# Channel vectors and x in one array: a changed order and size of the first transfers of an encoder trunk, and 25 warming products instead of 21

## The chip, the cores and the metric

The kernel runs on one core of a Trainium2 chip. The metric is the device time of one execution in microseconds (us); of several executions the median is given. A core has engines that run side by side, each with its own queue of instructions: TensorE (matrix products; PE in the profile, and PEld for the loading of its weights), VectorE (DVE), ScalarE (ACT), GpSimd (POOL) and SyncE (SP), which here issues nearly all transfers from device memory into on-chip memory (SBUF). The engines wait for each other and for transfers by semaphores.

## The reference, cut to what matters

Two layers of an encoder on x of 256 rows (T) by 1024 channels (D), all in float32. Each layer is

```
h = RMSNorm(x) * g_mix
[B_a | C_a | X_a | U_p | Q | K | V | Ga | Gp | Gt] = h @ W_in
y_a = W_a_out( B_a * conv3( C_a * X_a ) )
y_p = pool_scale * blockdiag( centred means of U_p  -  U_p )
y_t = W_attn_out( windowed attention of Q, K, V )
x   = x + W_o( sig(Ga)*y_a + sig(Gp)*y_p + sig(Gt)*y_t )
x   = x + W_down( silu(h2 W_gate) * (h2 W_up) ),  h2 = RMSNorm(x) * g_ffn
```

and a last RMSNorm follows. Six vectors of 1024 channels belong to a layer: g_mix, g_ffn, the three taps of the convolution, and pool_scale. They are the "channel vectors" of this document.

## The kernel before

The activations lie transposed: x is an array of 128 partitions by 8 blocks (k = 0 to 7) of 256 rows. The weights are cut into blocks of 128 by 128, put on the host into one long list `wst` in the order in which they are used, and stream in as chunks of 16 blocks (1 MB), with three buffers `raw`. Half a chunk (8 blocks) is converted at a time: ScalarE rounds it to the type fp32r (`hi`, L136), VectorE takes the rest (`lo`, L137). An activation is split in the same way. A block then costs three products on TensorE: hi by hi (L163), hi by the activation's rest (L164), the weight's rest by hi (L165). Each is 128x128 by 128x256.

The first products of the kernel are those for K and V of layer 0 (`quad_outer`, called first in `mixer`). Its loop runs over the eight k on the outside and four column blocks inside, so one k takes 4 blocks and 12 products, and all eight take 32 blocks (chunks 0 and 1) and 96 products. Q follows with chunk 2; the first of its eight column blocks is 24 products, and behind it stand the small products of the norm (L283). The activation that enters here is x times the channel vector g_mix (`xg_tiles`): `xg` is first rounded (on VectorE at L248 for k = 0 and 1, on ScalarE at L250 for the others) and then its rest is taken on VectorE (L251). The factor of the norm is multiplied in later. Beside that, the squares of x are taken on ScalarE (L257) and added on VectorE.

Before all this TensorE multiplies a tile of zeros WARM times (`wps`, L181), with no reader.

What sets the order: on SyncE the order of the code (`dma_chunk`); on the other engines a scheduler, from the code's order and its own costs. Chunk 0 and chunk 1 come in pieces with blocks of x between them (`dma_chunk`, `c < 2`); the channel vectors `ch` come first, in a transfer of their own. SyncE's transfers use eight semaphores in turn, so the ninth transfer waits, at its issue, until the first has landed, the tenth for the second, and so on.

## Time and profile before

| | |
|---|---|
| three executions | 980.19, 980.25 and 980.49 us; median 980.25 |
| the profiled execution | 981.37 us |
| its span, first to last instruction | 979.6 us, so 1.77 us lie around it |
| TensorE busy | 969.8 us, 99% of the span, 7877 products |
| VectorE, ScalarE, GpSimd busy | 711.9, 553.4, 41.4 us |
| granted clock of TensorE | 0.998 over the span |
| moved by transfers | 178.11 MB, mean 182 GB/s |
| last of the 21 warming products starts | at 5.6 us |
| first product that counts | starts at 7.21 us |

Times in the profile count from the first instruction. The rows of the timeline give the start, the duration, the engine, the line of the kernel, and what is written from what; a number behind x counts like rows merged into one, and what stands in brackets is how long the engine was idle before, and what it waited for. "SPq" is SyncE's queue of transfers: such a row is the issue alone, the transfer lands later.

### The profile page before, as it was taken

What the parts mean: (1) busy time and instruction counts of PE and PEld (TensorE: products, weight loads), DVE (VectorE), ACT (ScalarE), POOL (GpSimd) and SP (SyncE); (2) the same over time, 40 slices, a digit from 0 to 9 for tenths busy, and PEclk for the clock granted to TensorE, in tenths of its full rate; (3) what the DMA queues carried; (4) which work ended last, traced back from release to release, by engine and by line L of the source; (5) the groups of instructions that cost most, each with busy time, mean ns of one, the idle gap of its engine ahead of it and who ended that gap; (6) DMA issues with size and microseconds to landing.
All of it is one profiled execution on the core that took longest, in us unless ns stands there. A gap on an engine that the chain in (4) does not pass through costs nothing.

```text
span 979.6 us, 19115 instructions
## 1 busy us (share of the span) xinstructions
PE 969.8 (99%) x7877; PEld 956.7 (98%) x7877; DVE 711.9 (73%) x1277; ACT 553.4 (56%) x916; POOL 41.4 (4%) x60
## 2 busy tenths in 40 slices
PE   8999999999999999999999999999999999999997
PEld 8999999999999999999999999999999999999996
DVE  7899888667668955546589888975777697555555
ACT  5866676654456544444577566765554574444443
POOL 6000000000002000000020000000000020000000
PEclk9999999999999999999999999999999999999999
DMA  8656544555554555455543745444554455545531
GB/s 299 230 192 207 184 162 160 194 177 193 183 201 171 179 181 200 179 178 195 188 173 130 248 160 181 143 170 173 185 203 173 172 194 178 209 173 188 197 132 43
DMA packets 27399, 178.11 MB, mean 182 GB/s; under 512 B 3312, under 2 KB 4096, under 8 KB 7088
## 3 DMA queue, kind: packets, MB, share of 16 engines
q1 hardware_dynamic: 25200, 169.93, 48.7%
q0 software_dynamic: 2112, 6.97, 2.5%
q8 instruction: 61, 1.00, 0.4%
q14 instruction: 26, 0.21, 0.1%
HBM read 175.80 MB, written 1.08 MB: 181 GB/s over the span
## 4 chain that ended last, share of the span: by engine, by line
PE 98%; DMA 1%; DVE 0%; ACT 0%; SPq 0%; issue 0%; DVEq 0%
PE b L164 25%; PE b L163 25%; PE b L165 25%; PE dn L165 2%; PE dn L163 2%; PE dn L164 2%; PE dn L623 2%; PE dn L622 2%; PE dn L621 2%; PE wo L163 2%; PE wo L164 2%; PE o L395 2%; PE wo L165 2%; PE pt L380 1%; PE sc L351 1%; PE sc L352 1%
## 5 line engine op out<-in xcount | busy, mean ns | idle before, releaser
L137 DVE TENSOR_TENSOR lo<-raw,hi 128x1024 fp32r<-128x1024 f32 (+1 forms) x322 | 390.0, 1219 | 208.8 <-ACT hi L136 208.3
L136 ACT ACTIVATE hi<-raw 128x1024 fp32r<-128x1024 f32 (+1 forms) x322 | 337.2, 1052 | 331.0 <-PE b L164 212.5
L163 PE MATMUL b<-h,hi 128*128 128x256 f32 x1344 | 379.8, 283 | 0.0
L165 PE MATMUL b<-h,lo 128*128 128x256 f32 x1344 | 378.4, 282 | 0.0
L164 PE MATMUL b<-h,hi 128*128 128x256 f32 x1344 | 378.3, 281 | 0.0
L164 PEld LDWEIGHTS b<-h,hi 128*128 128x128 f32 x1344 | 253.2, 188 | 0.2
L163 PEld LDWEIGHTS b<-h,hi 128*128 128x128 f32 x1344 | 253.2, 188 | 0.2
L165 PEld LDWEIGHTS b<-h,lo 128*128 128x128 f32 x1344 | 253.1, 188 | 0.0
L163 PE MATMUL b<-xg,hi 128*128 128x256 f32 x448 | 127.7, 286 | 1.2 <-DVE xg L248 1.2
L164 PE MATMUL b<-xg,hi 128*128 128x256 f32 x448 | 127.5, 285 | 0.2 <-DVE xg L251 0.2
L165 PE MATMUL b<-xg,lo 128*128 128x256 f32 x448 | 127.3, 284 | 0.0
L163 PEld LDWEIGHTS b<-xg,hi 128*128 128x128 f32 x448 | 85.6, 191 | 1.4 <-issue 1.4
L164 PEld LDWEIGHTS b<-xg,hi 128*128 128x128 f32 x448 | 85.7, 191 | 0.5 <-DVE xg L251 0.5
L165 PEld LDWEIGHTS b<-xg,lo 128*128 128x128 f32 x448 | 85.6, 191 | 0.0
L165 PE MATMUL dn<-fa,lo 128*128 128x256 f32 x176 | 49.5, 281 | 0.0
L164 PE MATMUL dn<-fa,hi 128*128 128x256 f32 x176 | 49.5, 281 | 0.0
L163 PE MATMUL dn<-fa,hi 128*128 128x256 f32 x176 | 49.5, 281 | 0.0
L364 ACT ACTIVATE s<-s,sm 128x256 f32<-128x256 f32 x64 | 31.8, 498 | 12.7 <-DVE sm L359 12.7
L163 PE MATMUL b<-z,hi 128*128 128x256 f32 x128 | 36.4, 284 | 0.0
L165 PE MATMUL b<-z,lo 128*128 128x256 f32 x128 | 36.1, 282 | 0.0
L165 PE MATMUL b<-ao,lo 128*128 128x256 f32 x128 | 36.0, 282 | 0.0
L163 PE MATMUL b<-ao,hi 128*128 128x256 f32 x128 | 36.0, 281 | 0.0
(176 smaller groups left out, 1496.6 us busy)
## 6 DMA issues: line engine op xcount, KB each, us to landing
raw<-wst SPq DMA_DIRECT2D x158, 1024.0 KB, 4.9
bias<-stab POOLq DMA_DIRECT2D x16, 384.0 KB, 4.2
raw<-wst SPq DMA_DIRECT2D x4, 256.0 KB, 5.5
raw<-wst SPq DMA_DIRECT2D x2, 512.0 KB, 6.2
out<-yg SPq DMA_DIRECT2D x4, 256.0 KB, 2.2
x<-xT SPq DMA_DIRECT2D x4, 128.0 KB, 5.4
x<-xT SPq DMA_DIRECT2D x2, 256.0 KB, 6.3
gf<-gfin POOLq DMA_DIRECT2D x2, 256.0 KB, 3.5
```

Source lines behind the costliest of these rows:

```text
L136: S.activation(hi[:, s], raw[:, s], AF.Copy)
L137: V.tensor_tensor(lo[:, s], raw[:, s], hi[:, s].bitcast(F32), op=ALU.subtract)
L163: PE.matmul(dst, wh, xh, start=start, stop=False, skip_group_check=skip)
L164: PE.matmul(dst, wh, xl, start=False, stop=False, skip_group_check=skip)
L165: last_mm[0] = PE.matmul(dst, wl, xh, start=False, stop=stop, skip_group_check=skip)
L351: PE.matmul(ps[:, half(j)], qs[t][j][:, cs], kh, start=True, stop=False)
L352: PE.matmul(ps[:, half(j)], qs[t][j][:, cs], kl, start=False, stop=True)
L364: S.activation(ss[i // 2][:, i % 2], ss[i // 2][:, i % 2], AF.Exp, bias=sm[:, 4 + i:5 + i], accum_out=sm[:, 12 + i:13 + i])
L395: PE.matmul(ps[:, half(j)], vv, pts[kt][i][:, half(j)], start=(kt == i == 0), stop=(kt == i == 1))
L621: PE.matmul(d, ah[:, cs], wh, start=(k == 0), stop=False)
L622: PE.matmul(d, ah[:, cs], wl, start=False, stop=False)
L623: PE.matmul(d, al[:, cs], wh, start=False, stop=(k == FT - 1))
```

## The change

The six channel vectors of both layers (96 numbers to a partition) are laid in front of x in one array on the host, and in one tile `xc` on the chip; `ch` and `x` become views of it. The transfer of `ch` falls away: the first transfer now brings the channel vectors and x for k = 0 together (352 numbers to a partition, 176 KB), and it is issued ahead of the first weights. The first half of chunk 0 still comes in two transfers of 4 blocks. Its second half comes in one transfer of 8 blocks instead of two of 4, and x for k = 2 and 3 in one transfer instead of two. WARM goes from 21 to 25.

```diff
+NG = L * 6 * KT
...
     def dma_chunk(c):
         raw = wp.tile([P, CT * P], F32, name=f"raw{c}", tag="raw", bufs=3)
         if c < 2:
-            if c == 0:
-                nc.sync.dma_start(ch, chp)
-            for a, b, xa, xb in (((0, 4, 0, 1), (4, 8, 1, 2), (8, 12, 2, 3), (12, 16, 3, 4)),
-                                 ((0, 8, 4, 6), (8, 16, 6, 8)))[c]:
+            for a, b, xa, xb in (((0, 4, 0, 1), (4, 8, 1, 2), (8, 16, 2, 4)), ((0, 8, 4, 6), (8, 16, 6, 8)))[c]:
+                s = slice(0 if xa == 0 else NG + xa * T, NG + xb * T)
+                if xa == 0:
+                    nc.sync.dma_start(xc[:, s], xT[:, s])
                 nc.sync.dma_start(raw[:, a * P:b * P], wst[c, :, a * P:b * P])
-                nc.sync.dma_start(x[:, xa:xb], xT[:, xa:xb])
+                if xa > 0:
+                    nc.sync.dma_start(xc[:, s], xT[:, s])
...
-    x = act.tile([P, KT, T], F32, name="x")
-    ch = const.tile([P, L, 6, KT], F32, name="ch")
+    xc = act.tile([P, NG + KT * T], F32, name="x")
+    ch = xc[:, :NG].rearrange("p (l g k) -> p l g k", l=L, g=6)
+    x = xc[:, NG:].rearrange("p (k t) -> p k t", k=KT)
...
-WARM = 21
+WARM = 25
...
+    xT = np.ascontiguousarray(np.concatenate([chp.reshape(P, NG), xT.reshape(P, KT * T)], axis=1))
```

SyncE's queue from the start of the program, before. `raw0` and `raw1` are the buffers of chunks 0 and 1; in "128x512" the second number is elements to a partition, so 128x512 is 256 KB and 128x256 is 128 KB.

```order
L120 DMA ch_104<-chp 128x96
L123 DMA raw0_105<-wst 128x512
L124 DMA x_103<-xT 128x256
L123 DMA raw0_105<-wst 128x512
L124 DMA x_103<-xT 128x256
L123 DMA raw0_105<-wst 128x512
L124 DMA x_103<-xT 128x256
L123 DMA raw0_105<-wst 128x512
L124 DMA x_103<-xT 128x256
L123 DMA raw1_115<-wst 128x1024
L124 DMA x_103<-xT 128x512
```

The same queue now:

```order
L123 DMA x_107<-xT 128x352
L124 DMA raw0_108<-wst 128x512 x2
L126 DMA x_107<-xT 128x256
L124 DMA raw0_108<-wst 128x1024
L126 DMA x_107<-xT 128x512
L124 DMA raw1_115<-wst 128x1024
L126 DMA x_107<-xT 128x512
L124 DMA raw1_115<-wst 128x1024
L126 DMA x_107<-xT 128x512
```

x for k = 0 has moved ahead of the first weights, and two transfers of 4 blocks with x between them have become one of 8 blocks; up to the first chunk of full size there are 9 transfers of x and weights in place of 13 with `ch`.

ScalarE at the same place, before. `hi0` is the first half of chunk 0, `hi1` its second half, `hi2` the first half of chunk 1; `xg3` and `xg4` belong to k = 2 and 3, `xg5` to k = 4.

```order
L136 ACTIVATE hi0_154<-raw0_105 128x512 x2
L257 ACTIVATE sq9_198<-x_103 128x512
L136 ACTIVATE hi1_166<-raw0_105 128x512
L250 ACTIVATE xg3_172<-x_103,ch_104 128x256
L136 ACTIVATE hi1_166<-raw0_105 128x512
L250 ACTIVATE xg4_175<-x_103,ch_104 128x256
L257 ACTIVATE sq10_200<-x_103 128x512
L136 ACTIVATE hi2_178<-raw1_115 128x1024
L250 ACTIVATE xg5_182<-x_103,ch_104 128x256
```

ScalarE now:

```order
L138 ACTIVATE hi0_154<-raw0_108 128x512 x2
L261 ACTIVATE sq9_198<-x_107 128x512
L138 ACTIVATE hi1_166<-raw0_108 128x512 x2
L254 ACTIVATE xg3_172<-x_107 128x256
L254 ACTIVATE xg4_175<-x_107 128x256
L261 ACTIVATE sq10_200<-x_107 128x512
L138 ACTIVATE hi2_178<-raw1_115 128x1024
L254 ACTIVATE xg5_182<-x_107 128x256
```

Both pieces of `hi1` now stand ahead of `xg3`, since both come with the one transfer. On VectorE the same pairs have changed places, and the rest of `xg1` (k = 0) now stands ahead of the first `lo0`.

TensorE, the first products, before (`b14` and `b15` are banks of sums, `xg1` is k = 0):

```order
L181 MATMUL wps_81<-warm_75 128x256 x21
L163 MATMUL b14_232<-xg1_160,hi0_154 128x256
L163 MATMUL b15_233<-xg1_160,hi0_154 128x256
L164 MATMUL b14_232<-xg1_160,hi0_154 128x256
L165 MATMUL b14_232<-xg1_160,lo0_155 128x256
```

TensorE now:

```order
L183 MATMUL wps_81<-warm_75 128x256 x25
L165 MATMUL b14_232<-xg1_160,hi0_154 128x256
L166 MATMUL b14_232<-xg1_160,hi0_154 128x256
L167 MATMUL b14_232<-xg1_160,lo0_155 128x256
L165 MATMUL b14_232<-xg1_160,hi0_154 128x256
```

The second product of k = 0 is now the one with the activation's rest, and the third the one with the weights' rest `lo0`. Further down the engines' orders are as before, product for product.

## The prediction

> **What bounds the kernel now.** I read the page first (busy times and the chain that ended last), then the chain of waits in the first 20 us, then the timeline there engine by engine.

> ```profile
> span 979.6 us, 19115 instructions
> PE 969.8 (99%) x7877; PEld 956.7 (98%) x7877; DVE 711.9 (73%) x1277; ACT 553.4 (56%) x916; POOL 41.4 (4%) x60
> PE 98%; DMA 1%; DVE 0%; ACT 0%; SPq 0%; issue 0%; DVEq 0%
> ```

> TensorE is the bound from end to end; 98% of the chain is its products. The edits touch nothing behind the first two chunks, and no product that counts is added or removed. So the change is worth what it moves the moment at which TensorE is through with K and V of layer 0; whatever is gained there is carried to the end, since the products behind it stand in the same order and follow each other without a wait. That moment is found so:

> ```profile
> 1.19 4.85 PE L181 MATMUL wps<-warm 128*128 128x256 f32 x21 [1.19 <-DVE epst L176]
> 7.21 0.76 PE L163 MATMUL b<-xg,hi 128*128 128x256 f32 x2 [1.17 <-DVE xg L248]
> 24.71 0.50 PE L283 MATMUL ps<-ones,s 128*128 128x1 f32 x4
> ```

> ```profile
> 1.66 4.95 DMA x<-xT
> 6.71 0.06 DVE xg L248
> 6.98 0.68 DVE lo L137
> 7.66 0.44 DVE xg L251
> 8.14 0.58 PE b L164
> 8.73 0.21 PE b L165
> ...
> 13.63 0.21 PE b L165
> 13.84 0.12 PE b L163
> 13.96 0.12 PE b L164
> ```

> ```profile
> 8.14:13.80 5.66, 5.66 (x27) 5.66 (x27) 5.24 (x10) 5.46 (x11) 5.60 (x14) 1.00 1.04 394
> 13.80:24.70 10.90, 10.90 (x94) 10.90 (x93) 9.06 (x12) 6.43 (x9) 5.58 (x11) 1.00 0.89 334
> ```

> The second fence is the chain of waits (start, duration, what), the third the busy times in two stretches (the first number in brackets counts products; the last three columns are granted clock, share of the transfer engines, GB/s). Two products stand at 7.21; from 8.14 on products follow without a gap: 27 at 0.21 us up to 13.8, then at 0.119 (10.9 us for the remaining 91 of the 118 that stand ahead of L283). The column of granted clock shows 1.00 in both; the spacing is the better witness: TensorE is slow until 13.8 and runs at nearly twice the pace after it. The 96 products of K and V end 24 products ahead of the 24.71, at 24.71 - 24 x 0.119 = 21.86. At full pace from 7.7 (8.14 less the two early products at 0.21) they would have ended at 19.1. So the slow start costs 2.7 us here, the late start some more.

> **What the engines ahead of TensorE do.** SyncE, then ScalarE, then VectorE:

> ```profile
> 0.74 0.39 SPq L120 DMA_DIRECT2D ch<-chp  x1
> 1.19 0.42 SPq L123 DMA_DIRECT2D raw<-wst  x1
> 1.66 0.42 SPq L124 DMA_DIRECT2D x<-xT  x1
> ...
> 5.01 0.70 SPq L123 DMA_DIRECT2D raw<-wst  x1
> 6.62 0.33 SPq L124 DMA_DIRECT2D x<-xT  x1
> 7.50 0.33 SPq L123 DMA_DIRECT2D raw<-wst  x1
> 7.87 0.43 SPq L124 DMA_DIRECT2D x<-xT  x1
> 8.68 0.33 SPq L126 DMA_DIRECT2D raw<-wst  x1
> ```

> ```profile
> 5.02 0.63 ACT L136 ACTIVATE hi<-raw 128x512 fp32r<-128x512 f32 x1 [2.77 <-DMA raw<-wst]
> 7.50 0.63 ACT L136 ACTIVATE hi<-raw 128x512 fp32r<-128x512 f32 x1 [1.85 <-DMA raw<-wst]
> ...
> 8.68 0.63 ACT L136 ACTIVATE hi<-raw 128x512 fp32r<-128x512 f32 x1
> 9.22 0.51 ACT L250 ACTIVATE xg<-x,ch 128x256 fp32r<-128x256 f32 x1
> 9.84 0.63 ACT L136 ACTIVATE hi<-raw 128x512 fp32r<-128x512 f32 x1
> 10.38 0.49 ACT L250 ACTIVATE xg<-x,ch 128x256 fp32r<-128x256 f32 x1
> 10.78 0.61 ACT L257 ACTIVATE sq<-x 128x512 f32<-128x512 f32 x1
> 11.46 1.06 ACT L136 ACTIVATE hi<-raw 128x1024 fp32r<-128x1024 f32 x1
> ```

> ```profile
> 12.55 1.23 DVE L137 TENSOR_TENSOR lo<-raw,hi 128x1024 fp32r<-128x1024 f32 x1 [0.35 <-ACT hi L136]
> 13.69 0.88 DVE L251 SCALAR_TENSOR_TENSOR xg<-x,ch,xg 128x256 fp32r<-128x256 f32 x2
> ```

> SyncE's later issues wait for landings (the issue at 5.01 for the first weights, 6.62 for the first x, 7.50 the second weights, 7.87 the second x, 8.68 the third weights), so its rows are a list of landings. In bytes ahead and included: 304 KB landed at 5.01, 432 at 6.62, 688 at 7.50, 816 at 7.87, 1072 at 8.68; the fourth weights (1456) by 9.84, when ScalarE takes them.

> **The change, part by part.**

> *x ahead of the first weights, ch with it.* Before, TensorE's start hung on x (the chain's 4.95 us), since the weights had landed 1.6 us earlier. Now x leads and the weights R end the wait. R lies between 5.0 (they are issued at the same second place, near 1.2 us) and 6.6 (the same 432 KB had landed then). From R: hi 0.63, first product at R + 0.75; the first `lo` ends 0.68 later, so the third product starts near R + 1.4 and the stream runs as if begun at R + 1.0: 6.0 to 7.6. One issue of 0.39 us falls away, hidden in R.

> *Four more warming products.* The view of the tile `wps` gives the shortest, median and longest time of one in ns, and when the first and the last start:

> ```profile
> L181 PE MATMUL wps<-warm x21: 415/415/582, 1.2 to 5.6; 128*128 128x256 f32 x21
> ```

> They follow each other at the slow pace, 4 x 0.21 = 0.85 us: the last started at 5.6, so TensorE is free at 5.8 + 0.85 = 6.7. If R is 5.0 they hold the first product back by up to 0.9 us; if R is over 5.9 they cost nothing. Together: the stream begins as if at 6.7 to 7.6, 0.1 to 1.0 us before the old 7.7. I take the middle, 7.15.

> *The clock.* This is the unknown. Before, 4.85 us of warming products did not raise the pace, then TensorE was idle for 1.17 us, and 5.7 us after 8.14 the pace rose. Now it is busy from 1.19 to 6.7 and the gap behind is at most 0.65 us plus 0.3 at the third product. Bounds: the pace rises as early as 6.9 (1.19 + 5.7), if that gap counts for nothing, and as late as the old 13.8, if products of zeros count for nothing and the phase is that of before. I take early, since the stretch of 5.5 us is nearest to the 5.7 that sufficed.

> *The second half of chunk 0 in one transfer.* By itself this is a loss: ScalarE can begin only when all 8 blocks are there. Its landing L in bytes is 176 + 256 + 256 + 128 + 512 = 1328 KB, between 1072 at 8.68 and 1456 at 9.84: 8.68 + 1.16 x 256/384 = 9.45; I take 9.4, as there are fewer and larger transfers. Bounds are 8.7 (as early as the old third) and 10.4 (where ScalarE's old `xg4` shows the last x of this chunk landed). [...]

> From L the chain is ScalarE's and VectorE's. ScalarE has the same five instructions ahead of `hi2` as before (two hi, two xg, one squares); those took from 8.68 to 11.46 = 2.78, with short waits between them that one landing removes: 2.5. From `hi2` to the rest of `xg5` (k = 4) took 11.46 to 13.69 + 0.44 = 14.13: 2.67. So k = 4 can run from L + 5.2 on. Two hi-by-hi products go ahead, 48 products belong to k = 0 to 3, so 46 of the 96 remain: 46 x 0.119 = 5.5. End of K and V = L + 5.2 + 5.5 = L + 10.65. For k = 2 the same reckoning (one hi 0.63, two `lo` of 0.65 to 0.68, the rest of `xg3` 0.44, so L + 2.4, then 70 x 0.119 = 8.3) gives L + 10.7, the same: ScalarE and VectorE make work about as fast as TensorE takes it, so this chain sets the end once the pace is high. With L = 9.4 the end is 20.05.

> Against it TensorE alone: from 7.15 at high pace at once, 96 x 0.119 = 11.4, end 18.6; with the pace rising as late as 10.3, 15 slow products, then 81 x 0.119 = 9.6, end 19.95. Both are under 20.05, so the chain through L decides for any rise up to about 10.4, and neither R nor the exact moment of the rise matters then.

> *The third chunk*, next in line:

> ```profile
> 17.52 2.01 ACT L136 ACTIVATE hi<-raw 128x1024 fp32r<-128x1024 f32 x2 [1.09 <-DMA raw<-wst]
> 18.61 2.36 DVE L137 TENSOR_TENSOR lo<-raw,hi 128x1024 fp32r<-128x1024 f32 x2 [0.43 <-ACT hi L136]
> ```

> It landed at 17.5, and its first `lo` is there at 18.61 + 1.2 = 19.8. That was 2 us ahead of its use at 21.86; now it is 0.25 us ahead of 20.05. It is late next: unless it lands earlier too, the gain stops near 2.2. The bytes ahead of it are the same, so I leave it where it was.

> *Everything else* costs nothing: the views `ch` and `x` of one tile add no wait further down, and SyncE has four issues less, which its idle time hides.

> Sum: 21.86 - 20.05 = 1.8 us. Own time of the profiled execution 981.37 - 1.8 = 979.6; the median of the runs lies 1.1 us under that execution, so 980.25 - 1.8 = 978.45.

> **The rivals.** About 0.2%, or 1.96 us, is what a measurement of this kernel can tell from no change.

> 1. *The pace rises late all the same* (12.9 to 13.8: a gap at 6.7 to 7.3 starts the count anew, or zeros don't count). From 7.15, (13.8 - 7.15)/0.213 = 31 slow products, 65 x 0.119 = 7.7, end 21.5: gain 0.4 (0.75 with 12.9), time 979.5 to 980.1. For it: 4.85 us of zeros failed before. Against it: the gap has shrunk from 1.17 us, and the stretch has grown.
> A form of it is phase: were the moment of the rise drawn anew in each execution, the new times would spread from 978.45 to 980.0, and the three before would have spread by 1 us or more; they lie within 0.30 us, so this gets 0.05 of the chance below. [...]
> 2. *The 8 blocks land early*, near 8.7, and the third chunk 0.5 us early with them, because the queues fill sooner: end 19.35, gain 2.5, time 977.7; TensorE alone would allow 18.6, a gain of 3.2. For it: the five issues up to them, 0.47 us apart, are done by 3 us, where the eight for 1456 KB took until 4.4. Against it: the stretch up to 6.6 was slow with transfers queued (432 KB landed by then).
> 3. *Slower*: the one transfer of 8 blocks starves TensorE at k = 2. The place is ScalarE's `hi1`; the price is what L exceeds 11.2 (L + 10.65 against 21.86), and for 0.2% it must exceed 13.2, though 512 KB more than L's bytes and x had been taken at 11.46 before. Even a pace that falls back in the idle time ahead of k = 2 (about 1 us, 10.5 to 11.7) and rises again at 17 gives 26 slow products, end 22.4: 0.5 us more, within 0.2%.

> **Chances.** Early pace with L between 8.9 and 10.4 (gain 0.8 to 2.3): 0.65, and within it over 1.96 us at L under 9.25, which I put at somewhat under a half: 0.28. Late pace: 0.18, phase included. Early landing: 0.12. Slower by over 0.2%: 0.03; about even or slower by less: 0.02. Faster 0.28 + 0.12 = 0.40, slower 0.03, same 0.57. The range takes in most of the late pace and most of the early landing: 977.4 to 979.95.

> **What would show it.** Right: first product at 6.7 to 7.4, spacing 0.12 from there or soon after; a gap on TensorE ahead of k = 2 (row L166 waiting for VectorE's `xg`), ScalarE's two `hi` of 128x512 back to back near 9.4; the L283 row near 22.9. Wrong: spacing 0.21 beyond 12 us (the clock step fails), `hi1` far from 9.4 (the bytes), or the L283 row moved and the end not.

## The result, and the profile after

| | before | after |
|---|---|---|
| median of four executions each | 980.22 us (980.01 to 980.49) | 987.18 us (986.86 to 988.04) |
| profiled execution, its span | 981.37, 979.6 us | 987.34, 985.2 us |
| row of the norm's products (L283, now L287) | 24.71 us | 22.96 us |
| from that row to the end of the profiled time | 956.66 us | 964.38 us |

The ratio is 1.0072, 95% interval 1.0055 to 1.009: the change made the kernel slower by 7 us, where 1.8 us of gain were forecast.

The head of the page of after: TensorE is busy for 5.6 us more than before (969.8), with only four products more.

```profile
span 985.2 us, 19117 instructions
PE 975.4 (99%) x7881; PEld 963.1 (98%) x7881; DVE 712.6 (72%) x1277; ACT 553.5 (56%) x916; POOL 37.1 (4%) x60
```

The start is not where that went. First the timeline of TensorE in the kernel after, then that of ScalarE:

```profile
1.19 4.81 PE L183 MATMUL wps<-warm 128*128 128x256 f32 x25 [1.19 <-DVE epst L178]
5.84 0.30 PE L165 MATMUL b<-xg,hi 128*128 128x256 f32 x1
5.98 0.28 PE L166 MATMUL b<-xg,hi 128*128 128x256 f32 x1
...
10.62 0.50 PE L165 MATMUL b<-xg,hi 128*128 128x256 f32 x2
11.43 0.39 PE L166 MATMUL b<-xg,hi 128*128 128x256 f32 x1 [0.30 <-DVE xg L255]
11.65 0.28 PE L167 MATMUL b<-xg,lo 128*128 128x256 f32 x1
...
22.96 0.50 PE L287 MATMUL ps<-ones,s 128*128 128x1 f32 x4
```

```profile
5.07 0.63 ACT L138 ACTIVATE hi<-raw 128x512 fp32r<-128x512 f32 x1 [2.83 <-DMA raw<-wst]
...
9.02 1.15 ACT L138 ACTIVATE hi<-raw 128x512 fp32r<-128x512 f32 x2 [0.59 <-DMA raw<-wst]
10.07 0.90 ACT L254 ACTIVATE xg<-x 128x256 fp32r<-128x256 f32 x2
```

25 warming products now take 4.81 us, since the pace rose inside them (4.77 us by the starts of the single products); the first weights landed at 5.07, the 8 blocks at 9.02; TensorE waits a little ahead of k = 2 (11.43); and the L287 row stands 1.75 us ahead of the old one. The lead is then lost little by little. The view of one tile's products, the output projection of attention (`b<-ao`), shows it; its columns are the shortest, median and longest time of one in ns, then the first and the last start. Before, then after:

```profile
L163 PEld LDWEIGHTS b<-ao,hi x128: 187/188/189, 193.4 to 772.5; 128*128 128x128 f32 x128
L163 PE MATMUL b<-ao,hi x128: 279/281/285, 193.5 to 772.7; 128*128 128x256 f32 x128
```

```profile
L165 PEld LDWEIGHTS b<-ao,hi x128: 192/192/192, 193.2 to 778.4; 128*128 128x128 f32 x128
L165 PE MATMUL b<-ao,hi x128: 283/283/283, 193.3 to 778.5; 128*128 128x256 f32 x128
```

At 193 us the lead is down to 0.2, at 772 us it is a lag of 5.8. Nothing waits: a product takes 283 ns where the median was 281, a load of weights 192 where it was 188, and where the times varied before they are all equal now. The busy times in two stretches in the middle of the kernel (before, then after; the first number in brackets counts the products):

```profile
200.00:300.00 100.00, 100.00 (x842) 99.84 (x842) 68.62 (x115) 49.98 (x69) 0.00 (x0) 1.00 0.54 188
330.00:460.00 130.00, 130.00 (x1098) 130.00 (x1098) 74.97 (x82) 57.30 (x71) 0.00 (x0) 1.00 0.54 193
```

```profile
200.00:300.00 100.00, 100.00 (x833) 99.86 (x833) 68.37 (x114) 49.94 (x69) 0.00 (x0) 1.00 0.52 184
330.00:460.00 130.00, 130.00 (x1085) 130.00 (x1085) 74.24 (x82) 57.03 (x70) 0.00 (x0) 1.00 0.53 187
```

TensorE is never idle in either, the granted clock is 1.00 in both, yet 13 products fewer go through in 130 us. From start to start, a product takes 120.00 ns after, without exception in the second stretch; before, 115 to 122 ns in turn, mean 118.67. (All spacings below are such means of 330 to 460 us, from the starts of single products in the trace.) 1.33 ns on the some 7740 products behind the norm's row would be 10.3 us; the rows of the table above give 964.38 - 956.66 = 7.7, since other stretches lost less: the products of 128x256 lost 0.9 to 1.2 ns each at 30 to 60, 520 to 560 and 810 to 960 us. The last of these stretches lost nothing on the whole, for there stand also some 200 products of 128x512, the last layer's down projection, in which the activations are loaded and the weights are the other operand. They are 228 ns apart on the mean in place of 232, and the lag is 6.0 us at the start of that stretch and 5.9 at its end. The rows of the first of their three lines, before, then after:

```profile
L621 PE MATMUL dn<-hi,fa x88: 388/392/404, 806.3 to 971.4; 128*128 128x512 f32 x88
```

```profile
L625 PE MATMUL dn<-hi,fa x88: 389/389/396, 812.4 to 977.1; 128*128 128x512 f32 x88
```

7.7 less the 1.75 us of the start is the 5.97 between the two profiled executions; the medians differ by 7.0, since the profiled execution of before was slower than its median (below).

### The profile page after: what moved, and what is told of

The parts are those of the page before. It is cut to its first block, busy times and chain, and to the rows that moved or that the text cites. A ratio compares the mean times of both kernels' runs of the same rounds, so it can differ in the third digit from the quotient of the medians.

```text
span 985.2 us, 19117 instructions
## 1 busy us (share of the span) xinstructions
PE 975.4 (99%) x7881; PEld 963.1 (98%) x7881; DVE 712.6 (72%) x1277; ACT 553.5 (56%) x916; POOL 37.1 (4%) x60
## 4 chain that ended last, share of the span: by engine, by line
PE 98%; DMA 1%; DVE 0%; ACT 0%; SPq 0%; issue 0%
PE b L166 25%; PE b L165 25%; PE b L167 25%; PE dn L167 2%; PE dn L166 2%; PE dn L165 2%; PE dn L626 2%; PE dn L625 2%; PE dn L627 2%; PE wo L165 2%; PE wo L166 2%; PE o L399 2%; PE wo L167 2%; PE pt L384 1%; PE sc L356 1%; PE sc L355 1%
## 5 line engine op out<-in xcount | busy, mean ns | idle before, releaser
L165 PE MATMUL b<-h,hi 128*128 128x256 f32 x1344 | 381.5, 284 | 0.0
L166 PE MATMUL b<-h,hi 128*128 128x256 f32 x1344 | 380.2, 283 | 0.0
L167 PE MATMUL b<-h,lo 128*128 128x256 f32 x1344 | 380.2, 283 | 0.0
L166 PEld LDWEIGHTS b<-h,hi 128*128 128x128 f32 x1344 | 257.9, 192 | 0.2
L165 PEld LDWEIGHTS b<-h,hi 128*128 128x128 f32 x1344 | 257.8, 192 | 0.2
L167 PEld LDWEIGHTS b<-h,lo 128*128 128x128 f32 x1344 | 257.8, 192 | 0.0
L166 PE MATMUL b<-xg,hi 128*128 128x256 f32 x448 | 127.0, 284 | 0.8 <-DVE xg L255 0.8
L165 PE MATMUL b<-xg,hi 128*128 128x256 f32 x448 | 127.2, 284 | 0.3 <-DVE xg L252 0.3
L167 PE MATMUL b<-xg,lo 128*128 128x256 f32 x448 | 126.8, 283 | 0.2 <-DVE lo L139 0.2
L166 PEld LDWEIGHTS b<-xg,hi 128*128 128x128 f32 x448 | 85.9, 192 | 1.4 <-DVE xg L255 1.3
L165 PEld LDWEIGHTS b<-xg,hi 128*128 128x128 f32 x448 | 85.8, 192 | 0.6 <-issue 0.5
L167 PEld LDWEIGHTS b<-xg,lo 128*128 128x128 f32 x448 | 85.9, 192 | 0.4 <-DVE lo L139 0.4
L165 PE MATMUL dn<-fa,hi 128*128 128x256 f32 x176 | 49.8, 283 | 0.0
L166 PE MATMUL dn<-fa,hi 128*128 128x256 f32 x176 | 49.8, 283 | 0.0
L167 PE MATMUL dn<-fa,lo 128*128 128x256 f32 x176 | 49.8, 283 | 0.0
L165 PE MATMUL b<-z,hi 128*128 128x256 f32 x128 | 36.5, 285 | 0.0
L165 PE MATMUL b<-ao,hi 128*128 128x256 f32 x128 | 36.2, 283 | 0.0
L166 PE MATMUL b<-ao,hi 128*128 128x256 f32 x128 | 36.2, 283 | 0.0
L167 PE MATMUL b<-ao,lo 128*128 128x256 f32 x128 | 36.2, 283 | 0.0
```

Of the source, the lines that this page charges most:

```text
L165: PE.matmul(dst, wh, xh, start=start, stop=False, skip_group_check=skip)
L166: PE.matmul(dst, wh, xl, start=False, stop=False, skip_group_check=skip)
L167: last_mm[0] = PE.matmul(dst, wl, xh, start=False, stop=stop, skip_group_check=skip)
```

## The experiments

What could do that? The code of those products is unchanged. Two things differ: the phase in which the stream starts, and the places in SBUF. `ch` was a tile of 384 bytes to a partition in the pool `const`, which lies ahead of the weights' pool; taken out, all weights' tiles moved down by 384 bytes. The activations kept their addresses, since the 384 bytes came back at the head of `xc`, ahead of them. From the allocation of the compiled programs ("modulo 256" is what is left of a number of bytes when whole multiples of 256 are taken away; the difference of the two addresses, so reduced, is called the distance from here on):

| | `hi0` (weights) | `xg1` (activations) | activations minus weights, modulo 256 |
|---|---|---|---|
| before | 45152 | 108768 | 128 |
| after | 44768 | 108768 | 0 |

All `raw`, `hi` and `lo` tiles lie at one place modulo 256, and so do the activations' tiles that TensorE reads in its large products.

**Start or place.** Four kernels: after, with the 384 bytes put back into `const` unused, so that the weights are at their old addresses and the activations 384 further up (distance 0); before, with `ch` taken to where it lies after, and nothing else (distance 0); before with 25 warming products; after with 21.

```diff
+    pad = const.tile([P, NG], F32, name="pad")
+    V.memset(pad[:, 0:1], 0.0)
```

> The changed kernel with an unused tile of 384 bytes to a partition put where the channel vectors used to lie, so that raw, hi and lo stand at their old addresses (the activations behind x then stand 384 bytes further on). Theory 1 (the fast pace settles into one of two rhythms, 118.7 or 120.0 ns a product, by the way the stream starts, and addresses don't matter): 120.0 ns, about 987 us. Theory 2 (the weights' own addresses, moved by 384 bytes, cost 1.3 ns a product): 118.7 ns, 978.5 us. Theory 3 (the distance between the weights' and the activations' addresses): 120.0 ns, 987 us, as that distance is the changed kernel's.

```diff
+    ch = act.tile([P, L, 6, KT], F32, name="ch")
     x = act.tile([P, KT, T], F32, name="x")
-    ch = const.tile([P, L, 6, KT], F32, name="ch")
```

> The kernel before, with its transfers and its 21 warming products, but the tile of the channel vectors laid in front of x in the other pool: every tile then has the address that it has in the changed kernel. Theory 1 (rhythm by start): as before, 118.7 ns, 980.2 us. Theories 2 and 3 (addresses): 120.0 ns, 987 us plus the slow start of before, 989 us.

```diff
-WARM = 21
+WARM = 25
```

> The kernel before with 25 warming products and nothing else. All theories let the clock rise near 4.8 to 7 us. Theory 1 (rhythm by start): may fall into either rhythm; if into 120.0 ns, 985 to 988 us. Theories 2 and 3 (addresses): 118.7 ns, and 977.5 to 978.5 us from the early clock alone.

```diff
-WARM = 25
+WARM = 21
```

> The changed kernel with 21 warming products. Theory 1 (rhythm by start): may fall into either rhythm; if into 118.7, 977 to 979 us. Theories 2 and 3 (addresses): 120.0 ns, 986 to 988 us. The products that count were ready at 5.8 us, so fewer warming products by themselves give at most 0.5 us.

Measured, with the ratio to before and its 95% interval:

| | us | ratio | spacing, ns |
|---|---|---|---|
| after, weights back at their addresses (distance 0) | 987.10 | 1.0075 (1.006 to 1.009) | 120.00 |
| before, `ch` ahead of x (distance 0) | 987.42 | 1.0079 (1.0064 to 1.0094) | 120.00 |
| before, 25 warming products (distance 128) | 979.18 | 0.9996 (0.9987 to 1.0006) | 118.67 |
| after, 21 warming products (distance 0) | 987.04 | 1.0077 (1.006 to 1.0094) | 120.00 |

The stretch of 330 to 460 us in the second kernel, then in the third:

```profile
330.00:460.00 130.00, 130.00 (x1086) 130.00 (x1085) 74.98 (x84) 56.57 (x69) 0.00 (x0) 1.00 0.52 187
```

```profile
330.00:460.00 130.00, 130.00 (x1098) 130.00 (x1097) 74.19 (x81) 57.27 (x70) 0.00 (x0) 1.00 0.55 195
```

The second kernel has the old transfers and the old warming, and the whole loss. So the loss comes from moving `ch`, not from the start. The first shows that the weights' own address isn't it: at the old one they are as slow. What the slow kernels share is the distance of 0. Warming products, four more or fewer, do nothing that these runs can tell. The spacings came as theory 3 has them; the times that it gave for the second and the third kernel, 989 and 977.5 to 978.5 us, were missed, since both counted on more from the start than it was worth.

**The distance.** An unused tile ahead of `xc` moves the activations alone, by 128, 256, 384 and 64 bytes (32, 64, 96 and 16 numbers). The four expectations count the other way round, weights minus activations:

```diff
+    gap = act.tile([P, 32], F32, name="gap")
+    V.memset(gap[:, 0:1], 0.0)
     xc = act.tile([P, NG + KT * T], F32, name="x")
```

> The changed kernel with an unused tile of 128 bytes to a partition ahead of x: everything behind it (x, and all activations that TensorE reads) moves by 128 bytes, the weights don't. Distance of weights and activations modulo 512 is then 384, as in the kernel before (0 in the changed kernel and in the two slow ones with a moved layout). Theory 3a (the two operands' addresses modulo 256 must differ): 118.7 ns a product, 978.4 us. Theory 3b (modulo 512 must differ): the same. Theory 3c (each operand's own address counts, and only the old pair is good): 120.0 ns, 987 us.

> As the one with a gap of 128 bytes, but 256: distance 256 modulo 512, 0 modulo 256. Theory 3a: 120.0 ns, 987 us. Theory 3b: 118.7 ns or another rhythm below 120, 978 to 980 us. Theory 3c: 120.0 ns, 987 us.

> A gap of 384 bytes: distance 128 modulo 512. Theories 3a and 3b: below 120 ns, 978 to 980 us. Theory 3c: 120.0 ns, 987 us.

> A gap of 64 bytes: distance 448 modulo 512, 192 modulo 256, 64 modulo 128. If only whole steps of 128 bytes count (3a), half of the accesses would still meet: 119 to 120 ns, 981 to 987 us. Theory 3b: below 120 ns, 978 to 982 us. Theory 3c: 120.0 ns, 987 us.

With 128 bytes 979.71 us (ratio 0.9997, 0.9988 to 1.0006), with 256 986.85 (1.0071, 1.0055 to 1.0088), with 384 979.78 (0.9998, 0.9989 to 1.0008): the period is 256 bytes, and a distance of 128 gives back all of the loss. With 64 bytes 969.47 us came out, ratio 0.9888 (0.9874 to 0.9903), at 117.78 ns: none of the three theories had a time below 978 there, and the kernel before was not at its best either. The tile's view of that kernel:

```profile
L165 PEld LDWEIGHTS b<-ao,hi x128: 188/188/188, 188.4 to 760.9; 128*128 128x128 f32 x128
L165 PE MATMUL b<-ao,hi x128: 279/279/279, 188.5 to 761.0; 128*128 128x256 f32 x128
```

**Other distances, and each operand's own place.** 32 and 192 bytes by the same gap; 32 bytes in `const`, which moves weights and activations together onto multiples of 256 (distance 0); and the kernel before with a gap of 192, which makes its distance 128 + 192 = 320, that is 64.

> The changed kernel with an unused tile of 32 bytes a partition ahead of xc in `act`: all activations move up by 32 bytes, the weights stay. The distance activations minus weights is then 32 modulo 256. So far a distance of 0 gave 120.0 ns a product (987 us), 128 gave 118.67 ns (979.7 us) and 64 gave 117.78 ns (969.5 us). Theory A (the distance modulo 256 decides): not 120.0 ns, so clearly below 987 us; by the nearest distances 0 and 64, somewhere from 969 to 980 us, and below 969 if a smaller distance is better still. Theory B (the step counts in units of 64 bytes, and what lies within one unit counts as the same): 120.0 ns and 987 us, as with distance 0.

> The changed kernel with an unused tile of 192 bytes a partition ahead of xc in `act`: activations up by 192 bytes, weights as they are, distance 192 modulo 256, the mirror image of 64. Theory A (only how far apart the two are, either way round, counts): 117.8 ns a product and 969.5 us as with 64. Theory B (the direction counts, which operand runs ahead): another time than 969.5 by over 2 us, most likely between 970 and 980. Theory C (not the distance but the activations' own address gave 969.5): any time, since the activations' address is another than with 64.

```diff
+    gap = const.tile([P, 8], F32, name="gap")
+    V.memset(gap[:, 0:1], 0.0)
```

> The changed kernel with an unused tile of 32 bytes a partition in `const`, which lies ahead of weights and activations both: both move up by 32 bytes, the distance stays 0 modulo 256, and both now begin on whole multiples of 256 bytes instead of 32 below one. Theory A (the distance alone decides): 120.0 ns a product and 987 us, as the changed kernel. Theory C (each operand's own alignment counts beside it): another spacing, and a time that differs from 987 us by over 2 us.

> The kernel before, start and all, with an unused tile of 192 bytes a partition at the head of `act`: activations up by 192 bytes, weights as they are. Before, the distance was 128 modulo 256; now it is 320, that is 64. Theory A (the distance alone decides): 117.8 ns a product as in the changed kernel with distance 64, so 969.5 us plus what the old start costs, 0.2 to 0.8 us: 969.5 to 970.5 us. Theory C (the changed start is needed for the faster spacing, or the absolute addresses are): no change from 980 us, or any other time over 2 us away.

Both operands moved together: 987.00 us and 120.00 ns, as after. The kernel before at distance 64: 969.02 us, ratio 0.9893 (0.9876 to 0.9909), 117.78 ns, as the changed kernel at that distance. So at 0, 64 and 128 the distance decides, whichever start the kernel has; and the old start is no slower than the new one there (969.02 against 969.47). 32 bytes: 966.66 us (0.9866, 0.9851 to 0.988), so what lies within 64 bytes is not the same as 0. 192 bytes: 959.50 us, ratio 0.9795 (0.978 to 0.9809), not the 969.5 of its mirror image 64: the direction counts, and the 970 to 980 that were thought most likely in that case were too high. This is the fastest kernel of the study, 20 us under before. Its busy times in the same stretches, and the views of two of its tiles (`dn<-fa` is the second half of the FFN):

```profile
200.00:300.00 100.00, 100.00 (x849) 99.79 (x849) 70.84 (x122) 52.24 (x74) 1.30 (x1) 1.00 0.52 182
330.00:460.00 130.00, 130.00 (x1149) 130.00 (x1148) 76.30 (x84) 59.94 (x74) 0.00 (x0) 1.00 0.57 202
```

```profile
L165 PE MATMUL dn<-fa,hi x176: 276/276/276, 320.6 to 478.0; 128*128 128x256 f32 x176
```

```profile
L165 PE MATMUL b<-ao,hi x128: 281/281/281, 189.7 to 755.8; 128*128 128x256 f32 x128
```

In the second stretch the products start every 113.33 ns, but in the one from 200 us on 849 in 100 us are 117.8 each: at this one distance the stream runs for long stretches in one of two rhythms, each steady, and what chooses between them stays open.

**TensorE alone, and two more distances.** A bench ahead of the changed kernel's first product: 210 products of zeros for each of nine stretches, eight distances and the first once more, with the other engines at rest in most of it, in a single execution. And the gaps of 224 and 160 bytes.

```diff
+    for d in range(9):
+        for i in range(210):
+            b = i // 3 % 7
+            w = (th, th, tl)[i % 3][:, b * P + 8 * d:(b + 1) * P + 8 * d]
+            PE.matmul(wps[:, :T], w, tx[b][1 if i % 3 == 1 else 0], start=True, stop=True)
```

> The changed kernel with a bench ahead of its first real product: 9 x 210 products of zeros, weights from a `hi` and a `lo` tile, activations from 7 `xz` tiles, in the order of L165 to L167. The weights are read 32 bytes further on in each stretch of 210, so that the distance activations minus weights goes 0, 224, 192, 160, 128, 96, 64, 32, 0 modulo 256. Only the first stretch waits for anything; VectorE and ScalarE write none of these tiles meanwhile. Theory A (TensorE's own two reads make the spacing): stretches of 120.0 ns at distance 0, first and last, 118.7 at 128, 117.8 at 64, 116.7 at 32, 113 to 118 at 192. Theory B (the writes of ScalarE and VectorE beside it are needed for it): one spacing in all nine stretches. The total is the changed kernel's 987 us plus some 1890 x 0.117 = 220 us, and is not what is asked.

> The changed kernel with an unused tile of 224 bytes a partition ahead of xc: distance activations minus weights 224 modulo 256. Theory A (time falls as the activations lie less far below the next multiple of 256 from the weights): at or below the 959.5 us of 192. Theory B (192 is a minimum between 128, 979.7 us, and 256, 986.9 us): between 960 and 987 us, by the middle of 192 and 256 some 973.

> The changed kernel with an unused tile of 160 bytes a partition ahead of xc: distance 160 modulo 256. Theory A (time falls steadily from 128 to 192): half way between 979.7 and 959.5, some 969.6 us. Theory B (the time is the same in steps of 64 bytes): 979.7 as with 128, or 959.5 as with 192.

The busy times of the bench, one row for each stretch: 0, 224, 192, 160, 128, 96, 64, 32 and 0; VectorE and ScalarE (third and fourth column) stand still in all but the first and the last, and the transfers in all but the first:

```profile
8.00:31.00 23.00, 23.00 (x194) 23.00 (x193) 8.58 (x15) 4.83 (x7) 7.98 (x17) 1.00 0.70 253
32.00:56.00 24.00, 24.00 (x206) 24.00 (x205) 0.00 (x0) 0.00 (x0) 0.00 (x0) 1.00 0.00 1
57.00:80.00 23.00, 23.00 (x205) 23.00 (x204) 0.00 (x0) 0.00 (x0) 0.00 (x0) 1.00 0.01 1
81.00:105.00 24.00, 24.00 (x203) 24.00 (x202) 0.00 (x0) 0.00 (x0) 0.00 (x0) 1.00 0.01 1
106.00:130.00 24.00, 24.00 (x204) 24.00 (x204) 0.00 (x0) 0.00 (x0) 0.00 (x0) 1.00 0.00 1
131.00:155.00 24.00, 24.00 (x203) 24.00 (x202) 0.00 (x0) 0.00 (x0) 0.00 (x0) 1.00 0.01 1
156.00:180.00 24.00, 24.00 (x206) 24.00 (x206) 0.00 (x0) 0.00 (x0) 0.00 (x0) 1.00 0.01 1
181.00:204.00 23.00, 23.00 (x198) 23.00 (x197) 0.00 (x0) 0.00 (x0) 0.00 (x0) 1.00 0.00 1
206.00:229.00 23.00, 23.00 (x194) 23.00 (x193) 0.89 (x3) 0.59 (x2) 0.00 (x0) 1.00 0.01 1
```

By the starts of the products, beside the full kernels:

| activations minus weights, modulo 256 | 0 | 32 | 64 | 96 | 128 | 160 | 192 | 224 |
|---|---|---|---|---|---|---|---|---|
| TensorE alone, ns | 119.9 | 117.8 | 117.8 | 120.0 | 118.6 | 120.0 | 113.4 | 118.3 |
| full kernel, 330 to 460 us, ns | 120.0 | 116.7 | 117.8 | not run | 118.7 | 117.3 | 113.3 | 118.3 |
| full kernel, us | 986.9 to 987.4 | 966.7 | 969.0, 969.5 | not run | 979.2 to 980.2 | 974.6 | 959.5 | 976.8 |

At 0, 64, 128, 192 and 224 TensorE alone gives the spacing of the full kernel within 0.1 ns. So no write of another engine was needed for it there: VectorE and ScalarE are busy for 0.00 us in the rows of 224, 192, 128 and 64, and for 0.89 and 0.59 of 23 us in the second row of 0. This is what theory A, of TensorE's own two reads, expected; but it had 116.7 at 32, and the bench gave 117.8; at 160 the two differ by 2.7 ns, and the full kernel's six executions spread from 971.3 to 977.5 us. There something counts besides the distance, perhaps the order or the phase of the products; this stays open. 224 bytes: 976.77 us, ratio 0.9971 (0.9959 to 0.9983); 160 bytes: 974.59, 0.9947 (0.9927 to 0.9968). 192 is lower than both its neighbours, not a point of a slope. For 160 neither theory had it: the time lies between the 979.7 of 128 and the 969.6 half way to 192.

## Why the prediction was wrong, step by step

- *x ahead of the first weights, four more warming products.* The first weights landed at 5.07 (bounds 5.0 to 6.6), and the first product came at 5.84, ahead of the 6.7 to 7.4 forecast, since the warming products got faster inside their row.
- *The clock.* The early rise was taken, and it came: 4.77, earlier even than the bound of 6.9, which counted 5.7 us from 1.19. The reason given for the choice did not hold: the pace rose 3.6 us into the warming products here, and 3.3 us into those of the kernel before with `ch` moved, which has 21 of them, where it had not risen in the 4.85 us of the profiled execution of before. So the choice came right by luck, not by that reason.
- *The second half of chunk 0 in one transfer.* L was 9.02, for a forecast of 9.4. The gap ahead of k = 2 was there. The L287 row stood at 22.96, where 22.9 was forecast. That hit is partly luck: with L at 9.02 the forecast's own L + 10.65 is 19.7 for the end of K and V, and it came at 20.1 (22.96 less 24 products of 0.12), so a landing 0.4 early and a chain 0.4 longer cancelled. The third chunk's landing held nobody up.
- *"Whatever is gained is carried to the end, since the products behind it stand in the same order and follow each other without a wait."* This step failed. Order and waits are as assumed, but the spacing is not a constant of the product: with the layout it went from 118.67 to 120.00 ns.
- *"Everything else costs nothing: the views `ch` and `x` of one tile add no wait further down."* They add no wait; but moving `ch` out of `const` moved the weights against the activations, and the experiment that moved it alone has the whole loss. The mechanism was in no rival. The one on the slower side, 8 blocks that land late, had no part in it.
- *The size of the start's gain* was wrong too, against the median. With the layout's effect taken out (the changed kernel with the gap of 128 bytes, 979.71 us) the ratio is 0.9997 (0.9988 to 1.0006): at most 1.2 us of gain, not 1.8, and none that can be told from none. The term that was mis-sized is the old end at 21.86: the profiled execution of before, with its L283 row at 24.71, was of a late kind. In the two profiled executions the end of K and V did move by 1.8 us, from 21.86 to 20.1; but the same 1.8 was taken off the median, which lies 1.1 us under that execution. With the old transfers and 25 warming products that row stands at 22.67, and in the kernel before with the gap of 192, whose start is the old one in all, at 22.34.
- *Rival 1* has a slip in its time: gains of 0.4 to 0.75 us are 979.5 to 979.85, not 980.1. Its form by phase got 0.05, because three times lay within 0.30 us. 54 executions of before, across all comparisons, spread from 978.86 to 981.75 us. In the sixteen profiled executions of full kernels the trace's records of the granted clock begin with the rise: at 4.67 to 6.47 us in the twelve with 25 warming products, at 4.44, 6.04, 6.25 and, in the profiled execution of before, 13.71 in the four with 21. (Ahead of its first record the column of granted clock shows 1.00 at the slow pace too; so it did for the stretch of 8.14 to 13.8 us that the prediction read, with products 0.21 us apart.) So the rise stands at no fixed time from the start, not even among the twelve. The lengths of the records in which the clock is 1.00 share a step: 3.41 us for the short one in the kernel before with `ch` moved, 962.56 for the long one of before and 976.21 for that of after, which are 282 and 286 times 3.41333. On these records the form by phase should have had far more weight than three nearly equal times allowed it.

## What to carry to other kernels

An edit that moves a tile between pools is an edit of the layout: before costing it at nothing, compare the addresses of TensorE's two operands in the two compiled programs, modulo 256 (here a distance of 0 in place of 128 cost some 7 us). Here, with TensorE busy for 99% of the span, a spacing of 120.00 ns in place of 118.67 went with 7.7 us lost behind the start, where the start had gained 1.75; a count of products in a stretch of the middle (1085 in place of 1098 in 130 us) showed it when neither idle time nor granted clock did. A few unused bytes ahead of one operand's pool are a cheap thing to try: here 192 of them took 2.1% off the time (0.9795, 0.978 to 0.9809), where all the start edits together took off none that could be told.

## What the runs showed of the hardware

```profile
1.19 4.19 PE L181 MATMUL wps<-warm 128*128 128x256 f32 x21 [1.19 <-DVE epst L176]
7.14 0.47 PE L163 MATMUL b<-xg,hi 128*128 128x256 f32 x2 [1.76 <-DVE xg L248]
8.08 0.58 PE L164 MATMUL b<-xg,hi 128*128 128x256 f32 x1 [0.46 <-DVE xg L251]
8.46 0.41 PE L165 MATMUL b<-xg,lo 128*128 128x256 f32 x1
8.67 0.41 PE L163 MATMUL b<-xg,hi 128*128 128x256 f32 x1
```

```profile
4.44:7.85 3.41, 1.41 (x10) 1.03 (x9) 1.21 (x3) 1.08 (x2) 0.93 (x2) 1.00 0.89 297
7.86:11.26 3.40, 3.18 (x15) 3.18 (x16) 3.35 (x8) 3.27 (x7) 3.34 (x8) 0.50 1.05 381
11.27:20.00 8.73, 8.73 (x74) 8.73 (x74) 8.34 (x13) 7.65 (x13) 6.31 (x13) 1.00 1.03 406
```
